# A hybrid decoder layer on one core: where attention's masks, evictions, second q layout and matmul order are placed

## The chip, the cores and the metric

The kernel runs on one core of a Trainium2 chip. The metric is the device time of one execution in microseconds (us): 2123.47 us is the median of three runs of the kernel before (2120.73 to 2124.99). Every number that explains the time comes from one more execution, taken with the hardware profiler.

The engines are named as in the profile: PE is TensorE (matmuls), PEld its weight loads, DVE is VectorE, ACT is ScalarE, POOL is GpSimd, SP is SyncE, which here issues DMAs. SPq, POOLq and so on are the queues of these engines. L1547 is line 1547 of the kernel's source.

## The reference

One decoder layer over 2048 positions of width 1024. The part that matters here is the attention half of the mixer: 8 heads of 64, each with three causal branches of 128-key windows at dilation 1, 4 and 16, which are combined by their softmax denominators.

```python
h = rms_norm(x, g_mix); z = h @ w_in            # 1024 -> 3072
u, gb, gc, q, k, v = split(z)                   # six parts of 512
y_conv = gb * short_conv(gc * u, conv_w)        # depthwise, width 3
q = rms_norm(q, g_q) * 64 ** -0.5; k = rms_norm(k, g_k)
for window, dil in ((128, 1), (512, 4), (2048, 16)):
    # query t attends to keys t, t - dil, ..., t - window
    o[g], lse[g] = softmax_attention(...)
y_attn = sum_g softmax_g(lse)[g] * o[g]
x = x + concat(rms_norm(y_conv), rms_norm(y_attn)) @ w_out
h = rms_norm(x, g_ffn)
x = x + (silu(h @ w_gate) * (h @ w_up)) @ w_down     # 1024 -> 2816 -> 1024
```

All inputs are float32. The kernel splits each operand of a matmul into a high and a low float16 part and adds three products (high x high, high x low, low x high).

## The kernel before

**Stages.** First x is normalised, split and transposed, and one quarter of the convolution's channels is done (0 to 104 us of the profiled execution). Then comes the projection to q, k and v (`project`, to 370 us): four groups g of two heads, four units of 512 positions each, four PSUM banks a unit. Then attention (to about 730 us), with the other three quarters of the convolution and the first two pairs of the output projection threaded between its matmuls; then the output stage (`out_b`, to about 900 us), and the feed-forward part (to the end).

**Projection.** A unit fills four banks with 48 matmuls of 192 columns each (L1249). ScalarE copies each bank to `f` (L1264), squares, and casts v; VectorE and GpSimd normalise (L1304 to L1316); `qkhl` receives the high and low parts (L1319 to L1322), and one DMA writes it to `d_qk` (L1323). `qkhl` and the scratch `row` exist once. The banks come from the pool `cvx`, four banks in turn; the pool `psmm` with three more serves the convolution (and later the output) and is idle here. Beside this, ScalarE, VectorE, GpSimd and SP prepare the weights of later stages (`operands`, `spill_conv`, `spill_out`).

**Attention.** For each pair of heads, `load_pair` reads q, k-high and k-low with twelve transposing DMAs. Then for each head come three branches b in the order 1, 2, 0 (dilations 4, 16, 1). A branch has 16 query tiles of 128, taken four at a time; a step is one PSUM bank of scores, of up to four 128 x 128 blocks with keys on the partitions. Branches 0 and 1 need two steps for four query tiles, branch 2 one: 160 steps in all. In a step TensorE computes the scores (L1534); for b < 2 VectorE adds a mask to the bank (L1539; -1e30 where the band excludes a pair); ScalarE takes the exponential into `sm` (L1541); for b = 2 GpSimd zeroes the excluded half of it with one select (L1543); ScalarE casts to float16 (L1546), VectorE subtracts to get the low part (L1547), both into `et`; TensorE multiplies with v (AV, L1552) into the bank `av`. After four query tiles ScalarE copies `av` to the tile `u` (L1556, L1559). Branches 1 and 2 write `u` to DRAM and read it back in the order of positions as `r` (L1566 to L1571); when branch 0 is done, `combine` adds the three and divides (L1487 to L1495, on GpSimd but for the last head) and writes `d_y`.

Branches 1 and 2 take q in another order of positions, the tile `q16`. `regroup` makes it from the loaded q with four GpSimd copies a head (L1445).

**Order.** The source is written in program order; a planner then puts each engine's instructions into its queue. It runs a simulated clock with costs of its own, and gives each free engine the earliest-written instruction that is ready on that clock, so a later-written one may go first. Engines run their queues strictly in order on the chip. `issue_after(ins)` adds an edge: what the block issues on the engine of `ins` stands behind `ins` in its queue. `attention_pairs` interleaves: after step n of attention it takes 1.95 steps from `fill` (one step is three 512-column matmuls of the convolution or output projection, with the vector work between), and holds them behind the AV matmuls of step n - 12. Where scores and AV stand between these is left to the planner.

**Output stage.** It runs in eight pairs p of position tiles. `out_a(p)` loads x of two tiles into a slot `xk` and adds the convolution's half of the output projection (L599, L602); `tiles(p)` adds the other half (L660), stores the sum (L663) and prepares the feed-forward input. `out_a(p + 2)` stands ahead of `tiles(p)` in the program. The slots are two tiles named `qT` and two named `kb`; p = 1, 4, 7 use `kb`, the others `qT`.

Of the kernel before, what the change touches and what calls it, by code (L numbers as in the profile page):

```python
# [18 lines left out]
P = 128  # L19
# [7 lines left out]
HD = 64  # L27
# [3 lines left out]
class Builder:  # L31
# [170 lines left out]
    def run(self):  # L202
        tc, nc, A = self.tc, self.nc, self.A
        with ExitStack() as ctx:
# [16 lines left out]
            self.dmin = cp.tile([P, 11], F32, name="dmin")  # L221
# [350 lines left out]
    def out_a(self, p):  # L572
# [8 lines left out]
        xk = self.qk.tile([P, 2, D], F32, name="kb" if p % 3 == 1 else "qT")  # L581
# [429 lines left out]
class Fast(Builder):  # L1011
# [6 lines left out]
    PLAIN = 4  # L1018
# [16 lines left out]
    def in_and_conv(self):  # L1035
# [3 lines left out]
        self.d_wc = [dr.tile([P, 3, 2, KC, P], F16, name=f"d_wc{j}") for j in range(3)]  # L1039
        self.d_qk = [dr.tile([S, 6 * P], F16, name=f"d_qk{g}") for g in range(4)]  # L1040
        with ExitStack() as c:
            e = c.enter_context
            self.tmp = e(tc.tile_pool(name="tmp", bufs=3))
            s0 = e(tc.tile_pool(name="s0", bufs=2))
# [40 lines left out]
            self.sums_of = [None] * 4  # L1085
            wanted = [(c, t) for c in range(4) for t in range(2)] if self.PLAIN < 4 else []
            n = -1
            for step in self.conv_steps(0, W, before):
# [3 lines left out]
                if n == 6:  # L1092
                    norms.close()
                    with tc.issue_after(self.act.ins):
                        nc.scalar.preload_act_table_set("natural_log_exp_and_others")
                    self.ring = e(tc.tile_pool(name="ring", bufs=8, side="right"))
                    with tc.issue_after(self.dve.ins), tc.issue_after(self.sp.ins):
                        Wn = self.operands(0)
                elif self.PLAIN == 1 and n in (8, 10):
                    with tc.issue_after(self.dve.ins):  # L1100
                        self.sums(*wanted.pop(0), s0)
# [5 lines left out]
            for g in range(4):  # L1107
                Wg = Wn
                for i in range(4):
                    with ExitStack() as behind:  # L1110
                        for m in self.marks:
                            behind.enter_context(tc.issue_after(m))
                        if g < self.PLAIN:
                            for _ in range(2 if self.PLAIN == 1 else 1):
                                if wanted:
                                    self.sums(*wanted.pop(0), s0)
# [10 lines left out]

    def sums(self, c, t, s0):

        nc = self.nc
        pool, name = ((s0, "s0"), (self.qk, "qT"), (self.qk, "ka"), (self.qk, "kb"))[c]
        if t == 0:
            self.sums_of[c] = [pool.tile([P, 2, 2, 4, 256], F16, name=name, bufs=2) for _ in range(2)]
        Sc = self.sums_of[c]
        xh, xl = self.x[c]
        y = []
        for i in range(2):
            o = slice((t + 2 * i) * P, (t + 2 * i + 1) * P)  # L1140
            y.append(self.tmp.tile([P, KC, P], F32, name="t4"))
            nc.gpsimd.tensor_tensor(y[i], xh[:, :, o], xl[:, :, o], op=ALU.add)
        a11, a12, a21, a22 = (y[i][:, 4 * k:4 * k + 4] for i in range(2) for k in range(2))
        v = nc.vector
        v.tensor_tensor(a22, a21, a22, op=ALU.add)
        v.tensor_tensor(a21, a11, a21, op=ALU.subtract)
        v.tensor_tensor(a11, a22, a11, op=ALU.subtract)
        v.tensor_tensor(a12, a12, a11, op=ALU.subtract)
        for i in range(2):
            src = y[i].rearrange("p (a k) t -> p a k t", a=2)  # L1150
            hi, lo = (Sc[i][:, :, q, :, t * P:(t + 1) * P] for q in range(2))
            nc.scalar.copy(hi, src)
            v.tensor_tensor(lo, src, hi, op=ALU.subtract)

    def operands(self, g):
# [18 lines left out]
        W = [None] * 7  # L1174
# [6 lines left out]
        p = nc.gpsimd  # L1181
        if g < self.PLAIN:
            for n, x in ((0, b11), (1, b21), (2, b12), (3, b22)):
                split(n, x)
            return W
        split(0, b11)
        p.tensor_tensor(b11, b12, b11, op=ALU.subtract)
        split(2, b22)
        p.tensor_tensor(b12, b22, b12, op=ALU.subtract)
        p.tensor_tensor(b22, b22, b11, op=ALU.subtract)  # L1190
        split(5, b22)
        split(4, b11)
        split(1, b21)
        p.tensor_tensor(b21, b21, b22, op=ALU.subtract)
        split(6, b12)
        split(3, b21)
# [26 lines left out]
    def project(self, g, c, W):  # L1223
# [5 lines left out]
        Sc = self.sums_of[c]  # L1229
# [9 lines left out]

        def s_(i, a, t):  # L1240
            return lambda q, k: Sc[i][:, a, q, k, t * P:(t + 1) * P]
# [16 lines left out]
        if g < self.PLAIN:  # L1258
            for i in range(2):
                for h in range(2):  # L1260
                    ps = self.cvx.tile([P, 512], F32, name="cvx")[:, 0:384]
                    for k in range(2):
                        product(ps, lambda t: x_(i, 4 * k, t), W[2 * h + k], k == 0, k == 1)
                    nc.scalar.activation(block(i, h), ps, AF.Copy, scale=u)  # L1264
                last_squares() if i == 0 else None
        else:
            pool, name = ((self.psmm, "mm"), (self.cvx, "cvx"))[self.units % 2]
            self.units += 1
            ps = [pool.tile([P, 512], F32, name=name)[:, 0:384] for _ in range(3)]
            f11, f12, f21, f22 = (block(i, h) for i in range(2) for h in range(2))  # L1270
            left = (lambda t: x_(0, 0, t), lambda t: x_(0, 4, t), lambda t: s_(0, 1, t), lambda t: x_(1, 4, t),
# [663 lines left out]
```

## Time and profile before

| | |
|---|---|
| median of three runs | 2123.47 us (2120.73 to 2124.99) |
| the profiled execution | 2120.25 us, span 2118.5 us |
| TensorE busy | 2024.2 us (96%), 13368 matmuls |
| VectorE busy | 1354.1 us (64%) |
| ScalarE busy | 1031.3 us (49%) |
| GpSimd busy | 686.1 us (32%) |
| mean granted TensorE clock | 0.989 |

A row of a group of instructions reads: line, engine, operation, output <- inputs, shapes, count | busy us, mean ns of one | idle us of the engine just before them, and what ended that idle time. A row of waits reads: engine, tile and line <- who was waited for: us in total, times, longest. A row of a timeline reads: start us, length, engine, line, operation, count, and in brackets the idle time before it and what ended it.

### The profile page before, as it was taken

The numbers are of one execution on the slowest core, as the hardware profiler recorded it, in microseconds if no ns is written. First come the engines' busy times: TensorE is split into PE (matmuls) and PEld (weight loads), VectorE is DVE, ScalarE is ACT, GpSimd is POOL, SyncE is SP. The second block draws the span as 40 slices with busy tenths as digits, with TensorE's granted clock in tenths as the row PEclk, the third lists the DMA queues.
The fourth block names the chain that finished last, engine by engine and source line by source line (L and its number), as shares of the span: only waits on it lengthen the run. The fifth ranks groups of instructions, "written<-read, shape, count | busy, mean of one in ns | idle before, by whom it ended". The sixth has DMA issues, their size and how long they took to land. (4 is left out here: it accounts for less than half of the span.)

```text
span 2118.5 us, 34421 instructions
## 1 busy us (share of the span) xinstructions
PE 2024.2 (96%) x13368; PEld 1122.3 (53%) x13368; DVE 1354.1 (64%) x2487; ACT 1031.3 (49%) x1876; POOL 686.1 (32%) x574
## 2 busy tenths in 40 slices
PE   3999989999998898989999999999999999999998
PEld 2499989566656543434444444444444444444443
DVE  7454453577778867876767676676668575555463
ACT  7446564677777666553434333334333344343341
POOL 0024556334433212222211212231223245555463
PEclk9999999999999999999999999999999999999999
DMA  9658955357856577995323223322332762431442
GB/s 243 151 147 197 225 167 165 101 157 152 181 156 202 152 209 237 252 287 152 119 100 105 86 89 105 115 85 95 110 100 90 273 238 60 140 119 56 149 139 82
DMA packets 460157, 317.00 MB, mean 150 GB/s; under 512 B 255568, under 2 KB 413264, under 8 KB 457808
## 3 DMA queue, kind: packets, MB, share of 16 engines
q1 hardware_dynamic: 442304, 291.56, 49.7%
q10 hardware_dynamic: 17680, 23.16, 3.1%
q8 instruction: 106, 1.74, 0.3%
q14 instruction: 67, 0.55, 0.1%
HBM read 157.96 MB, written 116.85 MB: 130 GB/s over the span
## 5 line engine op out<-in xcount | busy, mean ns | idle before, releaser
L812 PEld LDWEIGHTS <-w 128*128 128x128 f16 x3696 | 362.0, 98 | 452.1 <-issue 17.6
L812 PE MATMUL ps<-b,w 128*128 128x512 f16 x2112 | 466.4, 381 | 11.0 <-DMA b<-d_h 5.2
L945 PE MATMUL ps<-b,w 128*128 128x512 f16 x1848 | 399.7, 379 | 2.9 <-DVE x L953 1.6
L812 PE MATMUL ps<-hb,w 128*128 128x512 f16 x1584 | 347.1, 379 | 0.0
L945 PEld LDWEIGHTS <-w 128*128 128x128 f16 x1848 | 180.6, 98 | 221.8 <-issue 4.0
L1249 PE MATMUL cvx<-w,b 128*128 128x192 f16 x3072 | 256.7, 247 | 8.6 <-ACT f L1264 8.4
L1249 PEld LDWEIGHTS <-b 128*128 128x128 f16 x3072 | 255.4, 98 | 9.9 <-issue 9.3
L705 POOL TENSOR_TENSOR t<-wq 128x512 f32<-128x512 f32 (+1 forms) x46 | 59.7, 1297 | 411.1 <-issue 175.8
L818 DVE TENSOR_TENSOR s<-ps,s 128x512 f32<-128x512 f32 x220 | 150.0, 682 | 36.6 <-PE ps L812 36.1
L952 POOL TENSOR_TENSOR x<-x,s 128x512 f32<-128x512 f32 x72 | 102.9, 1430 | 170.3 <-DVE s L966 132.0
L1547 DVE TENSOR_TENSOR et<-sm,et 128x512 f16<-128x512 f32 (+1 forms) x160 | 128.3, 820 | 36.2 <-ACT et L1546 35.0
L1541 ACT ACTIVATE sm<-s,bound,kap 128x512 f32<-128x512 f32 (+1 forms) x160 | 116.7, 754 | 45.1 <-DVE s L1539 37.7
L953 DVE SCALAR_TENSOR_TENSOR x<-ps,a_u,x 128x512 f32<-128x512 f32 x96 | 71.8, 749 | 98.6 <-PE ps L945 72.1
L191 PE MATMUL mm<-b,wq 128*128 128x512 f16 x320 | 123.3, 385 | 0.0
L192 PE MATMUL mm<-b,wq 128*128 128x512 f16 x320 | 123.1, 385 | 0.0
L193 PE MATMUL mm<-b,wq 128*128 128x512 f16 x320 | 123.0, 384 | 0.0
L722 ACT CAST w<-t 128x512 f16<-128x512 f32 x88 | 53.7, 615 | 127.6 <-PE ps L812 62.0
L96 DVE TENSOR_REDUCE vm_a<-wq 128x1 f32<-128x2048 f32 (+2 forms) x32 | 77.3, 2416 | 52.0 <-DMA wq<-in_w_up_dram 24.4
L1552 PE MATMUL av<-v,et 128*128 128x65 f16 x1800 | 81.5, 194 | 19.1 <-DVE et L1547 12.8
L933 DVE TENSOR_TENSOR w<-t,w 128x512 f16<-128x512 f32 (+1 forms) x96 | 75.4, 802 | 36.7 <-ACT w L932 36.3
L1539 DVE TENSOR_TENSOR s<-s,mask 128x512 f32<-128x512 f32 (+1 forms) x128 | 79.5, 649 | 28.9 <-PE s L1534 24.2
L923 ACT ACTIVATE wq<-wq,asf 128x512 f32<-128x512 f32 x88 | 56.6, 711 | 84.9 <-DMA wq<-d_a 84.9
(290 smaller groups left out, 3206.4 us busy)
## 6 DMA issues: line engine op xcount, KB each, us to landing
d_a<-a ACTq DMA_DIRECT2D x88, 256.0 KB, 2.0
d_wd<-w SPq DMA_DIRECT2D x77, 256.0 KB, 2.0
wq<-d_a SPq DMA_DIRECT2D x64, 256.0 KB, 4.2
b<-d_wd SPq DMA_DIRECT2D x14, 1024.0 KB, 6.6
wq<-in_w_in_dram SPq DMA_DIRECT2D x24, 512.0 KB, 7.2
d_qk<-qkhl SPq DMA_DIRECT2D x16, 768.0 KB, 4.4
d_h<-hl SPq DMA_DIRECT2D x24, 512.0 KB, 3.2
wq<-in_w_gate_dram SPq DMA_DIRECT2D x22, 512.0 KB, 5.3
```

The lines of the kernel that those rows point to most:

```text
L191: self.pe = mm(ps, lhsT=lh(k), rhs=rh(k), start=k == ks[0], stop=False)
L192: mm(ps, lhsT=lh(k), rhs=rl(k), start=False, stop=False)
L193: mm(ps, lhsT=ll(k), rhs=rh(k), start=False, stop=k == ks[-1])
L812: nc.tensor.matmul(ps[self.BANK[n]], lhsT=w[:, x, k], rhs=b[:, y, k], start=first and k == 0 and q == 0, stop=k == 3 and q == 2, skip_grou ...
L818: nc.vector.tensor_tensor(t, x, y, op=ALU.add)
L945: nc.tensor.matmul(ps[self.BANK[n]], lhsT=L[n][:, x, f], rhs=B[n][:, f, y], start=first and f == 0 and q == 0, stop=f == n_f - 1 and q == ...
L952: nc.gpsimd.tensor_tensor(o, o, s_, op=ALU.add)
L1249: self.pe = nc.tensor.matmul(ps[:, 192 * t:192 * (t + 1)], lhsT=lh(x, k), rhs=w[:, y, k], start=start and t + k + q == 0, stop=stop and k ...
L1539: nc.vector.tensor_tensor(sp[:, 0:o], sp[:, 0:o], self.masks[b][:, 512 - o:512], op=ALU.add)
L1541: nc.scalar.activation(e, sp[:, 0:o], AF.Exp, scale=self.kap, bias=self.bound)
L1547: nc.vector.tensor_tensor(et[:, 1], e, et[:, 0], op=ALU.subtract)
L1552: self.pe_av = nc.tensor.matmul(av[:, us.index(u)], lhsT=p_, rhs=v_, start=n_ == 0, stop=n_ == len(ops) - 1)
```

## The change

1. The projection's banks alternate between `cvx` and `psmm`, seven in turn.
2. x slots: odd pairs use `kb`, even pairs `qT`.
3. The unit's q part of `qkhl` is also written to a new DRAM tensor `d_q16` in the order of branch 2, with eight DMAs a unit; `load_pair` reads `q16` from it with four more transposing DMAs a pair. `regroup` goes.
4. The mask add on VectorE goes. After the exponential GpSimd zeroes the excluded entries of branches 0 and 1 with two selects a step, one over the blocks of each kind; the mask tiles and their preparation go.
5. VectorE copies `av` to `u` instead of ScalarE.
6. TensorE's order in attention is written out: scores of step n, AV of step n - 3, then the step's share of `fill`, each held behind the one before by `issue_after`. What follows a branch's last AV (store, read back, combine) moves with it. `et` has five buffers instead of four.
7. `combine` works on 8 query tiles at a time instead of 16, and stores `d_y` in halves; `dmin` has a column for each, `uv` two buffers.
8. Code that was not reached before (`PLAIN`, `sums` and the seven-product form of the projection) is removed.

```diff
-        xk = self.qk.tile([P, 2, D], F32, name="kb" if p % 3 == 1 else "qT")
+        xk = self.qk.tile([P, 2, D], F32, name="kb" if p % 2 else "qT")
...
+        for i in range(2):
+            for h in range(2):
+                pool, name = ((self.cvx, "cvx"), (self.psmm, "mm"))[self.units % 7 % 2]
+                self.units += 1
+                ps = pool.tile([P, 512], F32, name=name)[:, 0:384]
+                for k in range(2):
+                    product(ps, lambda t: x_(i, 4 * k, t), W[2 * h + k], k == 0, k == 1)
+                nc.scalar.activation(block(i, h), ps, AF.Copy, scale=u)
...
+        for a in range(8):
+            nc.sync.dma_start(self.d_q16[g].rearrange("(r c j a) e -> c a r j e", r=NT, c=4, j=4)[c, a],
+                              hl[16 * a:16 * a + 16, :, 0:2].rearrange("p j i x d -> p j (i x d)"))
...
-        st.setdefault("q16", [None, None])
...
+        st["q16"] = self.q16.tile([P, 2, NT, P], F16, name="q16", bufs=2)
+        for r in range(0, NT, 4):
+            self.transpose(st["q16"][:, :, r:r + 4].rearrange("p h r a -> p h (r a)"), self.d_q16[g][P * r:P * (r + 4)])
...
-                    if b < 2:
-                        nc.vector.tensor_tensor(sp[:, 0:o], sp[:, 0:o], self.masks[b][:, 512 - o:512], op=ALU.add)
...
-                    if b == 2:
-                        nc.gpsimd.affine_select(e, e, pattern=[[0, 4], [1, P]], compare_op=ALU.is_ge, fill=0.0, base=0,
-                                                channel_multiplier=-1)
-                    et = self.ep.tile([P, 2, 512], F16, name="et", bufs=4)[:, :, 0:o]
+                    bl = e.rearrange("p (n c) -> p n c", c=P)
+                    d0 = o // P % 2
+                    for m, sg in ((bl, 1),) if b == 2 else ((bl[:, 1 - d0::2], 1), (bl[:, d0::2], -1)):
+                        pattern = [[0, m.shape[1]], [sg, P]]
...
+                        nc.gpsimd.affine_select(m, m, pattern=pattern, compare_op=ALU.is_ge, fill=0.0, base=0,
+                                                channel_multiplier=-sg)
+                    et = self.ep.tile([P, 2, 512], F16, name="et", bufs=5)[:, :, 0:o]
...
-                    nc.scalar.copy(Ub[:, us[0]:us[0] + 4], av)
+                            nc.vector.tensor_copy(Ub[:, us[0]:us[0] + 4], ps)
...
+                    late.append(output)
+                    self.turn = mark.ins
+                    if len(late) > 3:
+                        with self.tc.issue_after(self.turn):
+                            late.pop(0)()
+                        self.turn = self.pe_av.ins
+                    yield self.turn
...
-            for _ in self.attn_steps(g, sts[g], sts[g + 1]):
-                marks.append(self.pe_av.ins)
-                with self.tc.issue_after(marks[n - lag]) if n >= lag else nullcontext():
+            for mark in self.attn_steps(g, sts[g], sts[g + 1]):
+                with self.tc.issue_after(mark):
                     while done < self.RATE * (n + 1):
-                        next(fill, None)
+                        if next(fill, 0) != 0:
+                            self.turn = self.pe.ins
                         done += 1
```

`output` is the function that now holds AV, the eviction, the stores and `combine` of a step; it is called three steps later.

More of the change, by code (lines that the diff above doesn't have):

```diff
@@ L220, in run @@
             self.eps = cp.tile([P, 3], F32, name="eps")
-            self.dmin = cp.tile([P, 11], F32, name="dmin")
+            self.dmin = cp.tile([P, 18], F32, name="dmin")
             self.low = cp.tile([P, 1], F32, name="low")
@@ L1039, in in_and_conv @@
         self.d_wc = [dr.tile([P, 3, 2, KC, P], F16, name=f"d_wc{j}") for j in range(3)]
+        self.d_q16 = [dr.tile([S, 2 * P], F16, name=f"d_q16{g}") for g in range(4)]
         self.d_qk = [dr.tile([S, 6 * P], F16, name=f"d_qk{g}") for g in range(4)]
@@ L1257, in last_squares @@
                 self.squares(3, self.last, self.pstr.tile([P, 4], F32, name="tr"), False)
[L1258 to L1271, printed above, removed]
-                    lambda t: s_(1, 1, t), lambda t: s_(0, 0, t), lambda t: s_(1, 0, t))
-            def plus(o, bank, z):
-                nc.vector.scalar_tensor_tensor(o, bank, u, z, op0=ALU.mult, op1=ALU.add)
-            for m in self.ORDER:
-                product(ps[self.BANK[m]], left[m], W[m], m in (0, 5, 4), m in (1, 2, 3))
-                if m == 0:
-                    nc.scalar.activation(f21, ps[0], AF.Copy, scale=u)
-                elif m == 5:
-                    plus(f12, ps[1], f21)
-                elif m == 1:
-                    nc.scalar.activation(f11, ps[0], AF.Copy, scale=u)
-                    last_squares()
-                elif m == 6:
-                    plus(f22, ps[1], f21)
-                    plus(f22, ps[2], f22)
-                elif m == 3:
-                    plus(f21, ps[1], f21)
-                elif m == 2:
-                    plus(f12, ps[2], f12)
+        for i in range(2):
[6 more added lines that the diff above has]
+                nc.scalar.activation(block(i, h), ps, AF.Copy, scale=u)
+            last_squares() if i == 0 else None
         fi = f.rearrange("p h j d -> p (h j) d")
@@ L1465, in attn_steps, with combine @@
         nc = self.nc
-        uv = self.at.tile([P, 1], F32, name="uv")
+        uv = self.at.tile([P, 1], F32, name="uv", bufs=2)
         nc.vector.tensor_scalar_mul(uv, self.uq[:, g:g + 1], 2.0 ** 17)
-        U, R = {}, {}
+        U, R, late = {}, {}, self.late
         for h, b in [(h, b) for h in range(2) for b in (1, 2, 0)]:
             q, ka, kl = (st[x][:, h] for x in ("qT", "ka", "kl"))
-            q16 = st["q16"][h]
-            if (h, b) == (0, 2):
-                self.regroup(st, 1)
+            q16 = st["q16"][:, h]
             if (h, b) == (1, 1) and g < 3:
                 self.load_pair(g + 1, nx)
-            if (h, b) == (1, 0) and g < 3:
-                self.regroup(nx, 0)
             Vb = self.load_v(g, h, b)
             last = g == 3 and h == 1
-            def combine(c, n):
+            def combine(c, n, h=h, last=last):
                 ts = slice(c, c + n)
@@ L1575, in pools @@
+                    late.append(output)
+                    self.turn = mark.ins
+                    if len(late) > 3:
+                        with self.tc.issue_after(self.turn):
+                            late.pop(0)()
+                        self.turn = self.pe_av.ins
+                    yield self.turn
+        if g == 3:
+            for output in late:
+                output()
     def pools(self, e):
@@ L1585, in constants @@
         nc = self.nc
-        self.masks = []
-        for b in range(2):
-            mask = self.keep.tile([P, 512], F32, name=f"mask{b}")
-            nc.gpsimd.memset(mask, 0.0)
-            for x in range(4):
-                sg = 1 if x % 2 else -1
-                t = mask[:, x * P:(x + 1) * P].rearrange("p (x a) -> p x a", x=4)
-                pattern = [[32 * sg, 4], [sg, 32]] if b == 0 else [[sg, 4], [4 * sg, 32]]
-                nc.gpsimd.affine_select(t, t, pattern=pattern, compare_op=ALU.is_ge, fill=-1e30, base=0,
-                                        channel_multiplier=-sg)
-            self.masks.append(mask)
         self.kap = self.keep.tile([P, 1], F32, name="kap")
```

137 lines of the change are left out of this document (46 added, 91 removed).

## The prediction

> **What bounds the kernel now.** I cut the span into the kernel's stages first, then asked TensorE alone what it waited for. A row of the first view has the stretch, its length, and each engine's busy time with its instructions; the last columns are granted clock, DMA share and GB/s.
>
> ```profile
> 104.00:370.00 266.00, 257.41 (x3083) 256.26 (x3081) 124.57 (x259) 152.46 (x280) 126.80 (x114) 0.99 0.72 179
> 384.00:730.00 346.00, 323.78 (x3631) 212.93 (x3630) 265.28 (x460) 247.95 (x476) 117.10 (x94) 0.99 0.64 160
> 730.00:920.00 190.00, 179.22 (x808) 79.78 (x807) 146.94 (x296) 118.95 (x213) 41.43 (x38) 0.96 0.84 235
> 920.00:2119.00 1199.00, 1180.66 (x5452) 532.95 (x5450) 754.21 (x1293) 446.56 (x790) 388.24 (x303) 1.00 0.38 123
> ```
>
> TensorE sets the end in every stage: it is busy 257 of 266 us in the projection, 324 of 346 in attention, 179 of 190 in the output stage. The change adds and removes no matmul, so all it can give is idle time of TensorE and the slow clock behind it. The last row, over half of the span, is untouched by the diff. The view of who waited for whom, TensorE alone:
>
> ```profile
> PE av L1552 <- DVE et L1547: 12.8, 17, 2.7
> PE cvx L1249 <- ACT f L1264: 8.4, 4, 4.8
> PE mm L191 <- DVE qT L599: 7.0, 1, 7.0
> PE av L1552 <- ACT et L1546: 3.8, 8, 1.6
> ```
>
> Three places, then: the projection waits 8.4 us for a bank, attention 12.8 + 3.8 = 16.6 us for probabilities (of 346.0 - 323.8 = 22.2 us idle), the output stage once 7.0 us for a sum with x.
>
> **Seven banks.** TensorE's rows of the projection:
>
> ```profile
> 113.18 150.64 PE L1249 MATMUL cvx<-w,b 128*128 128x192 f16 x1824
> 277.25 33.87 PE L1249 MATMUL cvx<-w,b 128*128 128x192 f16 x384 [4.75 <-ACT f L1264]
> ```
>
> Undisturbed, 150.64 / 1824 = 0.0826 us per matmul; a bank takes 48, so 3.96 us, and four banks cover a ScalarE that is 16 us late, seven 28 us. The longest wait beyond four is 4.75 us, less than the 11.9 us that three banks add: all 8.4 us can go. After it 384 matmuls took 33.87 instead of 31.7 us: 2.1 us of slow clock. Together 10.5 us.
>
> **x slots by pair.** The output stage's rows, by TensorE, the DMA queue and GpSimd:
>
> ```profile
> 815.74 0.38 PE L192 MATMUL ps<-b,b 128*128 128x512 f16 x1
> ...
> 817.90 0.38 PE L193 MATMUL ps<-b,b 128*128 128x512 f16 x1
> 825.25 0.58 PE L191 MATMUL mm<-b,b 128*128 128x512 f16 x1 [6.97 <-DVE qT L599]
> ...
> 830.32 0.63 PE L191 MATMUL ps<-b,b 128*128 128x512 f16 x1
> ...
> 788.03 0.85 SPq L663 DMA_DIRECT2D d_x<-kb  x1
> ...
> 812.27 1.26 SPq L663 DMA_DIRECT2D d_x<-qT  x1
> ...
> 819.57 0.82 SPq L592 DMA_DIRECT2D qT<-in_x_dram  x2
> ...
> 823.38 2.28 POOL L602 TENSOR_TENSOR qT<-qT,xt 128x512 f32<-128x512 f32 x1 [20.46 <-DMA qT<-in_x_dram]
> ```
>
> The x of pair 5 goes into the slot of pair 2, which is stored at 812.27; the load is issued at 819.57, GpSimd and VectorE get it at 823.4, TensorE stands for 6.97 us. Then 12 matmuls take 830.32 - 825.25 = 5.07 us, where ten took 2.16 before: 2.5 us of slow clock, 9.5 us in all. By parity, pair 5 takes the slot of pair 1, whose last stores went out at 788, 24 us earlier, and from pair 4 on every load waits only for the pair four before it. Pair 7 loads later than now, behind pair 3's store, still a pair ahead of its use. VectorE is busy 147 of 190 us here, so something else may be late by a microsecond or two next: I take 8.0 of 9.5.
>
> **Masks, evictions.** Groups of attention's stretch, by line; behind the bar busy us, mean ns, idle before:
>
> ```profile
> L1541 ACT ACTIVATE sm<-s,bound,kap 128x512 f32<-128x512 f32 x120 | 91.1, 782 | 27.5 <-DVE s L1539 25.0 <-PE s L1534 1.8 <-DVE et L1547 0.3
> L1546 ACT CAST et<-sm 128x512 f16<-128x512 f32 x120 | 72.1, 624 | 2.4 <-POOL sm L1543 1.3 <-POOL cu L1405 0.5 <-PE av L1552 0.2
> L1539 DVE TENSOR_TENSOR s<-s,mask 128x512 f32<-128x512 f32 x88 | 58.9, 690 | 17.1 <-PE s L1534 16.6
> L1539 DVE TENSOR_TENSOR s<-s,mask 128x384 f32<-128x384 f32 x40 | 21.4, 557 | 11.8 <-PE s L1534 7.6 <-ACT et L1546 4.2
> L1559 ACT COPY u<-av 128x260 f32<-128x260 f32 x64 | 23.9, 375 | 18.1 <-PE av L1552 17.7
> L1445 POOL COPY q<-qT 128x512 f16<-128x512 f16 x24 | 29.6, 1276 | 5.2 <-PE s L1534 5.2
> L1543 POOL TENSOR_SCALAR_AFFINE_SELECT sm<-sm 128x512 f32<-128x512 f32 x32 | 21.8, 684 | 67.9 <-ACT sm L1541 60.2 <-DVE cg L1415 7.6
> L1487 POOL TENSOR_TENSOR r<-r,r 128x1040 f32<-128x1040 f32 x7 | 17.9, 2554 | 87.9 <-DMA r<-d_u 87.9
> L1488 POOL TENSOR_TENSOR u<-u,r 128x1040 f32<-128x1040 f32 x7 | 17.7, 2524 | 4.3 <-ACT u L1559 3.2 <-POOL r L1487 0.9
> L1495 POOL TENSOR_TENSOR u<-u,bm 128x1024 f32<-128x1024 f32 x7 | 14.3, 2049 | 18.8 <-DVE bm L1493 18.8
> L1405 POOL MEMSET cu<- 128x2 f32 x2 | 0.2, 92 | 0.0
> ```
>
> VectorE loses the mask adds, 58.9 + 21.4 = 80.3 us. It gains 96 evictions of 260 columns: from 690 and 557 ns for 512 and 384 columns, 1.04 ns a column, so 557 - 124 x 1.04 = 428 ns, 41 us (ScalarE's 375 ns is the other end, 36 us). Net -39 us of 265. ScalarE loses 96 x 0.375 = 36 of 248 us.
>
> GpSimd gains two selects for each of 128 score tiles. No row shows one of 256 columns: if all of 684 ns is width it is 0.34 us, if all is fixed 0.68. The memset of two columns, 92 ns, is the nearest to a fixed part: 0.092 + 0.592 / 2 = 0.39 us, 0.24 for 128 columns. So 88 x 0.78 + 40 x 0.63 = 94 us, less 29.6 us of regrouping copies: GpSimd goes from 117 to 181 of 346 us. No engine is full; the question is who waits for whom. GpSimd runs in order, and each combine (L1487, L1488, L1495, 49.9 us in seven) now stands between masks.
>
> GpSimd and VectorE also hold each other up. The timelines of GpSimd and VectorE:
>
> ```profile
> 601.95 2.58 POOL L1488 TENSOR_TENSOR u<-u,r 128x1040 f32<-128x1040 f32 x1
> ...
> 571.10 0.74 DVE L1411 SCALAR_TENSOR_TENSOR cg<-cu,convw,cg 128x512 f32<-128x512 f32 x1
> ...
> 596.84 0.68 DVE L1547 TENSOR_TENSOR et<-sm,et 128x512 f16<-128x512 f32 x1
> ...
> 602.22 2.87 DVE L1411 SCALAR_TENSOR_TENSOR cg<-cu,convw,cg 128x512 f32<-128x512 f32 x1
> ```
>
> L1411, 0.74 us elsewhere, takes 2.87 us and ends at 605.09, 0.56 us behind GpSimd's add (604.53). L1547's mean of 795 ns in the groups above its 0.68 us alone is the same. That is where TensorE's 16.6 us come from: the probabilities of a step stand behind a combine.
>
> The Trainium skill's page SBUF — State Buffer, in "Who interferes with whom", says that a VectorE instruction with two SBUF inputs and a GpSimd instruction that reads SBUF exclude each other for the whole instruction, and one with a single SBUF input is free. By it the mask add (PSUM and mask) never blocked, and the selects that replace it do. The row above agrees for an add on GpSimd, with 0.18 us of overlap; the price for selects is the third rival.
>
> **TensorE's order.** AV of a step now comes three steps behind its scores. A step is 346 / 160 = 2.16 us, so 6.5 us are there for exponential 0.78, two selects 0.78, cast 0.62, subtraction 0.68: 2.9 us, leaving 3.6 us. The longest wait for L1547 was 2.7 us, so the 16.6 us can go. The three half-combines (half of 2.55 + 2.52 + 2.05: 3.6 us) just fit; a little more wait for r or for L1493 does not. I charge 0.6 us for each of seven, 4.1 us: attention gains 12.5 us. Bounds: all 22.2 idle us and the 1% of clock missing there (3.5 us) on one side, the rivals on the other. The 5.6 us of other idle time I leave; three banks of scores and two of AV are reused after three and two steps, later than their 0.78 and 0.43 us need.
>
> **q stored twice.** Rows of the page's DMA part, then the DMA queue, then GpSimd and the queue at the end of the projection:
>
> ```profile
> d_qk<-qkhl SPq DMA_DIRECT2D x16, 768.0 KB, 4.4
> ...
> 406.31 2.91 SPq L1566 DMA_DIRECT2D d_u<-u  x4
> ...
> 473.98 6.12 SPq L199 DMA_TRANSPOSE qT<-d_qk  x4
> ...
> 354.80 8.91 POOL L1445 COPY q<-qT 128x512 f16<-128x512 f16 x8
> ...
> 385.75 1.31 POOL L1322 TENSOR_TENSOR qkhl<-row,qkhl 128x256 f16<-128x256 f32 x2
> ...
> 390.69 0.88 SPq L1455 DMA_DIRECT2D v<-d_v  x2
> ```
>
> Per unit eight more issues at 2.91 / 4 = 0.73 us or less: up to 5.8 us of a queue that serves a unit every 4 x 3.96 = 15.8 us, ahead of the weight loads and spills written behind them. They are hidden by the 28 us of banks; without that cover a late weight reduction costs up to 5.8 us each time. Four more transposes a pair cost 6.1 us of queue, a pair ahead of their use. At the end of the projection the v load of attention stands behind the last unit's stores (385.75 + 1.31, then 390.69), now up to 5.8 us more, while TensorE arrives 10 us sooner; against that GpSimd is rid of the 8.91 us of copies that held up the last two units. From 0 to 6 us of wait, near its lower end: 2.0 us, charged to the projection, which gives 8.5. uv, dmin, the tile of five, the halved d_y stores and the missing mask tiles touch nothing that waits.
>
> **Sum.** 8.5 + 8.0 + 12.5 = 29.0 us from the profiled execution's 2120.25 us (span 2118.5 and 1.75 around it): 2091.3. The median of the runs lies 3.2 us above that execution, so 2094.
>
> **Rivals.** (a) Attention gives nothing, since in-order queues trade one wait for another: 2094 + 12.5 = 2107. For it: GpSimd, ScalarE and VectorE become one chain. Against: 3.6 us of slack and less work on two of them. (b) Projection and x slots give nothing: 2094 + 16.5 = 2111. For it: DMA share 0.72 there and eight more stores a unit. Against: their causes are a bank and a slot. (c) Slower: selects and VectorE's two-input work take turns. In a step of branches 0 and 1 they need 2s + 0.68 + (49.9 + 24 x 0.74) / 160 = 2s + 1.10 us against TensorE's 323.8 / 160 = 2.02. At 0.39 us that is 1.88, just below; at 0.684 it is 2.47, so 128 x 2.47 + 32 x 2.02 = 381 us, 35 longer, less 16.5: 2142. It decides from 0.62 us on, where 363 us are reached. (d) Slower too: the planner puts the add of the r tiles (L1487) ahead of the masks of branch 0, where it waits 87.9 / 7 = 12.6 us for its DMA; each costs 12.6 - 3.6 = 9.0 us, 63 in all, less 16.6 and 16.5: 2153. It decides from 8.3 us of wait on. For it: that wait exists; against: only planned order can place it so early, and r is now planned later too.
>
> **Chances.** Forecast 0.61, (a) 0.15, (b) 0.10, (c) 0.08, (d) 0.06. The range goes from all gains (10.5 + 9.5 + 22.2 + 3.5 = 45.7 below 2123.5: 2078) to 2118, over (a) and (b), and leaves out (c) and (d). A change of 0.2%, 4.2 us, is what can be told: faster 0.81, same 0.07 (where (a) and (b) meet), slower 0.12.
>
> **What would show it.** Right: no wait of L1249 for L1264 over 1 us; no wait of L191 for L599; attention's stretch near 333 us; selects of 256 columns near 0.39 us. Wrong: AV waiting for et by more than 16 us in all, GpSimd idle behind r while masks queue, L1547's mean over 1 us, or the first AV waiting for v or for q's transposes.

## The result: slower, and where the time went

The changed kernel takes 2140.59 us, the kernel before 2122.1 us on the same chip: a ratio on record of 1.0091 (the two medians alone give 1.0087), with a 95% interval of 1.0079 to 1.0103. The forecast was 2094. The profiled executions are 2140.6 and 2118.5 us long, 22.1 us apart. The view by stretches, cut at five marks of TensorE (the projection's first and last matmul, the first and the last AV matmul, the first FFN matmul); a row has the stretch, its length, the busy time of TensorE, its weight loads, VectorE, ScalarE and GpSimd, then granted clock, DMA share and GB/s. The changed kernel:

```profile
103.80:368.20 264.40, 257.10 (x3081) 255.91 (x3081) 120.87 (x257) 150.01 (x274) 117.29 (x106) 0.99 0.76 190
368.20:408.50 40.30, 21.65 (x97) 10.08 (x96) 9.98 (x21) 15.01 (x30) 14.08 (x20) 0.75 0.67 168
408.50:754.50 346.00, 319.71 (x3598) 213.06 (x3597) 224.43 (x449) 221.64 (x370) 198.27 (x336) 0.97 0.65 158
754.50:918.40 163.90, 157.00 (x716) 70.24 (x716) 123.29 (x248) 98.63 (x179) 36.08 (x35) 0.99 0.77 231
```

The same marks in the kernel before:

```profile
104.10:370.10 266.00, 257.41 (x3082) 256.26 (x3081) 124.47 (x259) 152.46 (x280) 126.80 (x114) 0.99 0.72 179
370.10:393.40 23.30, 22.57 (x117) 11.08 (x116) 9.69 (x21) 11.39 (x25) 11.87 (x13) 1.00 0.44 119
393.40:728.80 335.40, 314.95 (x3578) 208.06 (x3577) 258.91 (x449) 242.42 (x466) 114.05 (x89) 0.98 0.64 159
728.80:895.40 166.60, 157.27 (x714) 70.35 (x715) 125.43 (x255) 99.94 (x182) 35.09 (x34) 0.97 0.80 227
```

Two stretches carry the loss. From the projection's end to the first AV it is 40.3 us instead of 23.3 (+17.0), with TensorE idle nearly half of it and its clock at 0.75. From the first to the last AV it is 346.0 instead of 335.4 (+10.6). Three stretches give little: projection -1.6, output stage -2.7, FFN -0.9 us (1222.2 and 1223.1); the first AV as a whole comes 15.1 us later. Six rows of TensorE's waits in the changed kernel say the same (total, times, longest; the waits before the projection are left out):

```profile
PE s L1448 <- DMA q<-d_q: 18.7, 1, 18.7
PE av L1475 <- DVE et L1465: 13.6, 12, 3.0
PE av L1475 <- ACT et L1464: 12.3, 7, 3.5
PE ps L812 <- ACT s L863: 5.5, 1, 5.5
PE mm L1194 <- ACT f L1210: 4.3, 3, 3.1
PE cvx L1194 <- ACT f L1210: 2.2, 2, 1.4
```

**Ahead of attention.** The first scores wait once, 18.7 us, for q16. The DMA queue and TensorE at that point:

```profile
388.55 2.99 SPq L1246 DMA_DIRECT2D d_q<-qkhl  x5
392.88 5.27 SPq L199 DMA_TRANSPOSE q<-d_q  x4
401.05 0.38 PE L1448 MATMUL s<-q,ka 128*128 128x256 f16 x1 [18.65 <-DMA q<-d_q]
```

The transposes of pair 0's q16 are issued behind the last unit's last stores, although pair 0's q was stored some 190 us earlier. The tile of q16 has doubled from two buffers of 4 KB a partition to two of 8 KB, and in the built program its pool now reaches over the memory of the projection's qkhl.

**In attention.** GpSimd, VectorE and TensorE around one of seven like places:

```profile
524.94 1.96 POOL L1461 TENSOR_SCALAR_AFFINE_SELECT sm<-sm 128x256 f32<-128x256 f32 x4
530.96 2.52 POOL L1400 TENSOR_TENSOR r<-r,r 128x520 f32<-128x520 f32 x2 [4.06 <-DMA r<-d_u]
533.43 0.77 POOL L1461 TENSOR_SCALAR_AFFINE_SELECT sm<-sm 128x256 f32<-128x256 f32 x2
534.88 1.12 DVE L1465 TENSOR_TENSOR et<-sm,et 128x512 f16<-128x512 f32 x1 [5.97 <-ACT et L1464]
534.91 0.30 PE L1475 MATMUL av<-v,et 128*128 128x65 f16 x4 [3.49 <-ACT et L1464]
521.92 0.41 SPq L1495 DMA_DIRECT2D d_u<-u  x1
526.71 0.37 SPq L1497 DMA_DIRECT2D r<-d_u  x1
```

GpSimd stands 4.06 us before the add of the r tiles, then does both halves (2.52 us), and only then comes the next mask, whose exponentials ScalarE had finished by 528.8 at the latest. AV runs three steps later now, so branch 2's u goes out at 521.92, its r is fetched from 526.71, and the add stands in GpSimd's order at about the time it lands. GpSimd's waits for r add up as follows:

```profile
POOL r L1400 <- DMA r<-d_u: 17.7, 7, 5.1
```

The evictions came out at their estimate (424 ns, 428 forecast), the selects above it: 486 and 412 ns in the mean for 256 and 128 columns where 0.39 and 0.24 us were forecast, so the new selects take 115 us in that stretch instead of 94 (its groups; mean ns behind the busy time):

```profile
L1461 POOL TENSOR_SCALAR_AFFINE_SELECT sm<-sm 128x256 f32<-128x256 f32 x213 | 99.3, 486 | 83.8 <-ACT sm L1453 80.1 <-DVE cg L1334 2.1 <-DVE et L1465 1.4
L1461 POOL TENSOR_SCALAR_AFFINE_SELECT sm<-sm 128x128 f32<-128x128 f32 x38 | 15.6, 412 | 0.0
L1483 DVE COPY u<-av 128x260 f32<-128x260 f32 x63 | 26.7, 424 | 13.6 <-PE av L1475 13.0
```

### The profile page after: what moved, and what is told of

Its sections match the earlier page's. It is cut to its first block, busy times and chain, and to the rows that moved or that the text cites. A ratio compares the mean times of both kernels' runs of the same rounds, so it can differ in the third digit from the quotient of the medians.

```text
span 2140.6 us, 34957 instructions
## 1 busy us (share of the span) xinstructions
PE 2027.0 (95%) x13368; PEld 1126.0 (53%) x13368; DVE 1320.6 (62%) x2483; ACT 1012.5 (47%) x1780; POOL 760.4 (36%) x809
## 4 chain that ended last, share of the span: by engine, by line
PE 65%; DMA 9%; DVE 7%; ACT 6%; SPq 5%; issue 4%; POOL 2%; DVEq 0%; ACTq 0%; POOLq 0%
PE ps L812 33%; PE ps L945 15%; SPq L199 3%; PE mm L191 3%; PE mm L192 3%; PE mm L193 3%; PE s L1448 2%; PE cvx L1194 2%; PE mm L1194 2%; PE av L1475 2%; DVE vm_a L96 1%; DMA nx_x<-in_x_dram 1%; DMA wq<-d_a 1%; DMA x<-d_x 1%; POOL sm L1461 1%
## 5 line engine op out<-in xcount | busy, mean ns | idle before, releaser
L812 PE MATMUL ps<-b,w 128*128 128x512 f16 x2112 | 465.9, 381 | 11.3 <-ACT s L863 5.5
L1461 POOL TENSOR_SCALAR_AFFINE_SELECT sm<-sm 128x256 f32<-128x256 f32 (+2 forms) x288 | 136.3, 495 | 143.2 <-ACT sm L1453 137.9
L1465 DVE TENSOR_TENSOR et<-sm,et 128x512 f16<-128x512 f32 (+1 forms) x160 | 121.2, 762 | 99.6 <-ACT et L1464 98.0
L1194 PE MATMUL cvx<-w,b 128*128 128x192 f16 x1776 | 151.2, 246 | 3.3 <-ACT f L1210 2.2
L1464 ACT CAST et<-sm 128x512 f16<-128x512 f32 (+1 forms) x160 | 93.8, 589 | 71.3 <-POOL sm L1461 70.2
L191 PE MATMUL mm<-b,wq 128*128 128x512 f16 x320 | 125.7, 393 | 0.0
L192 PE MATMUL mm<-b,wq 128*128 128x512 f16 x320 | 125.7, 393 | 0.0
L193 PE MATMUL mm<-b,wq 128*128 128x512 f16 x320 | 125.6, 392 | 0.0
L1194 PE MATMUL mm<-w,b 128*128 128x192 f16 x1296 | 113.0, 248 | 4.3 <-ACT f L1210 4.3
L1475 PE MATMUL av<-v,et 128*128 128x65 f16 x1800 | 85.4, 195 | 26.1 <-DVE et L1465 13.6
```

What stands on the lines that cost most here:

```text
L191: self.pe = mm(ps, lhsT=lh(k), rhs=rh(k), start=k == ks[0], stop=False)
L192: mm(ps, lhsT=lh(k), rhs=rl(k), start=False, stop=False)
L193: mm(ps, lhsT=ll(k), rhs=rh(k), start=False, stop=k == ks[-1])
L812: nc.tensor.matmul(ps[self.BANK[n]], lhsT=w[:, x, k], rhs=b[:, y, k], start=first and k == 0 and q == 0, stop=k == 3 and q == 2, skip_grou ...
L1194: self.pe = nc.tensor.matmul(ps[:, 192 * t:192 * (t + 1)], lhsT=lh(x, k), rhs=w[:, y, k], start=start and t + k + q == 0, stop=stop and k ...
L1461: nc.gpsimd.affine_select(m, m, pattern=pattern, compare_op=ALU.is_ge, fill=0.0, base=0, channel_multiplier=-sg)
```

## Experiments

For each run: the ratio to the kernel before with its interval, the times of the marks in its profiled execution (us from the span's start), and the sum of AV's waits for et.

| run | ratio (95%) | projection ends | first AV | last AV | first FFN matmul | AV waits for et |
|---|---|---|---|---|---|---|
| before | 1 | 370.1 | 393.4 | 728.8 | 895.4 | 16.6 |
| changed | 1.0091 (1.0079 to 1.0103) | 368.2 | 408.5 | 754.5 | 918.4 | 25.9 |
| e1 | 1.0057 (1.0043 to 1.0072) | 369.6 | 396.7 | 746.2 | 909.0 | 26.2 |
| e2 | 1.0050 (1.0036 to 1.0065) | 368.0 | 406.9 | 742.0 | 908.1 | 21.5 |
| e3 | 1.0005 (0.9996 to 1.0014) | 360.1 | 395.4 | 731.7 | 899.1 | 17.5 |
| e4 | 1.0000 (0.9990 to 1.0010) | 371.8 | 395.5 | 731.2 | 895.2 | 19.7 |
| e5 | 1.0006 (0.9996 to 1.0017) | 371.0 | 398.3 | 733.9 | 897.7 | 22.1 |
| e7 | 1.0156 (1.0134 to 1.0177) | 360.5 | 393.4 | 773.8 | 936.8 | 48.4 |
| e8 | 0.9983 (0.9973 to 0.9992) | 360.2 | 385.0 | 732.5 | 895.3 | 26.8 |
| e9 | 0.9865 (0.9846 to 0.9884) | 360.7 | 384.8 | 709.4 | 873.0 | 9.3 |
| e10 | 1.0047 (1.0030 to 1.0064) | 371.5 | 398.6 | 747.1 | 909.9 | 26.9 |
| e11 | 0.9876 (0.9859 to 0.9892) | 373.8 | 392.5 | 714.8 | 878.1 | 8.0 |
| e12 | 0.9995 (0.9984 to 1.0007) | 370.3 | 408.9 | 733.7 | 898.6 | 7.9 |
| e13 | 0.9881 (0.9864 to 0.9897) | 361.0 | 385.5 | 710.2 | 877.1 | 8.7 |

The FFN stage, which no run changes, lasts between 1218.2 and 1230.5 us in these executions; times of single executions are compared only by their marks up to there.

### e1: q16 over free memory

```diff
             early.close()
+            e(tc.tile_pool(name="pad", bufs=1)).tile([P, 3104], F32, name="pad")
             self.fq = e(tc.tile_pool(name="fq", bufs=1))
+            self.hlp = e(tc.tile_pool(name="hlp", bufs=1))
...
-        self.qkhl = self.fq.tile([P, 4, 6, 2, HD], F16, name="qkhl")
+        self.qkhl = self.hlp.tile([P, 4, 6, 2, HD], F16, name="qkhl")
```

> The changed kernel with q16's two buffers laid over memory that is free before the last unit of the projection (a pad behind tmp, qkhl above the other tiles of fq). Nothing else is moved. Theory: the first scores wait 18.7 us for q16 because its memory lies on qkhl, which the last unit still stores from; then the first scores start at 382 to 386 instead of 401, the first AV waits up to 5 us for v, and the kernel takes 13 to 19 us less: 2122 to 2128. Rival: the eight stores per unit hold up the DMA queue itself; then the first scores stay behind 395 and at most 6 us are gained: 2134 or more.

Measured: 2136.9 us beside 2124.93. The pad shifts the projection's other tiles of that pool too, but of these only qkhl shared memory with q16. The place in memory was the cause of that wait: the transposes go out from 364.7 us on and the first scores start at 384.3 instead of 401.1. But the first AV gains only 11.8 us and the kernel some 7 by the ratios, because the next wait is close behind. TensorE and ScalarE:

```profile
384.33 0.27 PE L1450 MATMUL s<-q,ka 128*128 128x256 f16 x1
394.92 0.37 PE L1450 MATMUL s<-q,ka 128*128 128x256 f16 x1 [6.19 <-ACT sm L1455]
391.38 0.71 ACT L1241 CAST qkhl<-row 128x256 f16<-128x256 f32 x2 [6.38 <-DMA d_q<-qkhl]
394.19 0.67 ACT L1455 ACTIVATE sm<-s,bound,kap 128x384 f32<-128x384 f32 x1 [0.36 <-DMA d_v<-vs]
```

Three banks of scores are full and wait for the first exponential, which stands in ScalarE's order behind the last unit's casts. Attention now waits for the tail of the projection on ScalarE.

### e2: the r-add later in GpSimd's order

```diff
-                e.tensor_tensor(X[1], X[1], X[2], op=ALU.add)
+                with self.tc.issue_after(self.sel):
+                    e.tensor_tensor(X[1], X[1], X[2], op=ALU.add)
...
-                        nc.gpsimd.affine_select(m, m, pattern=pattern, compare_op=ALU.is_ge, fill=0.0, base=0,
-                                                channel_multiplier=-sg)
+                        self.sel = nc.gpsimd.affine_select(m, m, pattern=pattern, compare_op=ALU.is_ge, fill=0.0, base=0,
+                                                           channel_multiplier=-sg).ins
```

> The changed kernel with the add of the r tiles (L1400) queued on GpSimd behind the masks of the third step of the next head. Theory: GpSimd stands for r's DMA (17.7 us in 7 waits) with masks queued behind it, and that is most of AV's 26.1 us of waiting for et; then that sum falls under 10 us, no wait of GpSimd for r is over 1 us, and the kernel takes 12 to 22 us less: 2118 to 2128. Rival: the combine's 7.8 us of GpSimd work a head doesn't fit between the masks wherever it stands; then the sum stays over 18 us and the gain is under 6 us: 2134 or more.

Measured: 2134.47 us beside 2124.93. The wait for r is as good as gone (one of 1.9 us), the stretch from first to last AV is 335.1 us instead of 346.0, but AV still waits 21.5 us. Both expectations were half right: the wait for r cost some 9 to 11 us, and what was left has another cause. VectorE and GpSimd at one place:

```profile
573.80 1.17 DVE L1405 TENSOR_SCALAR bm<-u 128x8 f32<-128x8 f32 x1
575.75 1.26 DVE L1405 TENSOR_SCALAR bm<-u 128x8 f32<-128x8 f32 x1
577.92 1.42 DVE L1466 TENSOR_TENSOR et<-sm,et 128x512 f16<-128x512 f32 x1
572.09 2.86 POOL L1402 TENSOR_TENSOR u<-u,r 128x520 f32<-128x520 f32 x2
575.72 1.26 POOL L1346 TENSOR_TENSOR sq<-sq,c 128x512 f32<-128x512 f32 x1
```

The two halves of the combine stand back to back on GpSimd, VectorE's small steps for both stand between two subtractions, and in each half one of them (L1405) ends only with the GpSimd instruction beside it. The subtraction for AV, whose cast was ready at 576.4 (ScalarE's row, 575.78 and 0.62 us), starts at 577.9 and takes 1.42 us.

### e3: seven banks alone

```diff
-                    ps = self.cvx.tile([P, 512], F32, name="cvx")[:, 0:384]
+                    pool, name = ((self.cvx, "cvx"), (self.psmm, "mm"))[self.units % 7 % 2]
+                    self.units += 1
+                    ps = pool.tile([P, 512], F32, name=name)[:, 0:384]
```

> The kernel before with the seven banks alone. The prediction's term: the waits for L1264 go and 8 to 10.5 us with them: 2112 to 2114 beside 2122. Theory now: the planner, which knows of seven banks, lets ScalarE's evictions fall behind by as many banks (the largest lag was 17 us in the kernel before, 29.7 us in the changed one), so that waits of 4 to 8 us stay: 2116 to 2122.

Measured: 2126.42 us beside 2124.93, no difference. Both expectations fell. The waits for L1264 did go (0.7 us in all is left) and the projection's matmuls end 10.0 us sooner, as the prediction had it. Then the gain is handed back. TensorE and ScalarE:

```profile
393.29 0.37 PE L1536 MATMUL s<-q,ka 128*128 128x256 f16 x1 [6.12 <-ACT sm L1543]
395.41 0.82 PE L1554 MATMUL av<-v,et 128*128 128x65 f16 x12 [1.11 <-DMA v<-d_v]
386.42 1.14 ACT L1322 CAST qkhl<-row 128x512 f16<-128x512 f32 x2 [0.64 <-POOL row L1318]
392.56 1.23 ACT L1543 ACTIVATE sm<-s,bound,kap 128x384 f32<-128x384 f32 x2 [0.48 <-DMA d_qk<-qkhl]
```

The first AV comes at 395.4, and at 393.4 in the kernel before. TensorE's 8.4 us of waits in the projection were slack: the last unit's way through ScalarE, GpSimd and the DMA queue is no shorter with more banks, it only lags TensorE by more (ScalarE ends the last eviction at 376.2 us, at 374.4 in the kernel before; from the end of a bank's last matmul to the start of its eviction the timelines show up to 23.9 us, 17.2 before).

### e4: x slots alone

```diff
-        xk = self.qk.tile([P, 2, D], F32, name="kb" if p % 3 == 1 else "qT")
+        xk = self.qk.tile([P, 2, D], F32, name="kb" if p % 2 else "qT")
```

> The kernel before with the x slots by parity alone. The prediction's term: the 7.0 us wait for L599 goes and 8.0 to 9.5 us with it: 2112 to 2114 beside 2122. Rival, from the changed kernel, whose output stage is 2.8 us shorter: another wait takes its place and 1 to 4 us are gained: 2118 to 2121.

Measured: 2125.72 us beside 2124.93, no difference. The wait of 7.0 us for L599 is gone, but the output stage is only 2.6 us shorter (five waits of 0.5 to 2.4 us in its place), and that goes too where the FFN starts. There the wait for the scale of L863 is longer; this run:

```profile
PE ps L812 <- ACT s L863: 5.5, 1, 5.5
```

The kernel before:

```profile
PE ps L812 <- ACT s L863: 2.1, 1, 2.1
```

### e5: e1 and e2 together (both diffs above)

> The changed kernel with both e1's place for q16 and e2's later r-add. Theory: the two losses lie in different stretches and add up: first AV at 396 to 398 us, last AV some 335 us later, 2122 to 2128, level with the kernel before. Rival: what is gained ahead of attention is lost in it again; then 2131 or more.

Measured: 2125.06 us beside 2124.46, level with before, as the theory had it. The two losses are in different places and add up.

### e7: q16 by GpSimd's copies again

```diff
-        for a in range(8):
-            nc.sync.dma_start(self.d_q16[g].rearrange("(r c j a) e -> c a r j e", r=NT, c=4, j=4)[c, a],
-                              hl[16 * a:16 * a + 16, :, 0:2].rearrange("p j i x d -> p j (i x d)"))
...
+            if (h, b) == (0, 2):
+                self.regroup(st, 1)
...
+            if (h, b) == (1, 0) and g < 3:
+                self.regroup(nx, 0)
```

> The changed kernel with q16 made by GpSimd's copies again (no second store of q, no transposes of it); banks, x slots, masks and order as changed. Theory: the first AV comes when the last unit's chain through ScalarE, GpSimd and the DMA queue is through, at 393 to 397 us with or without seven banks, so 15 us of the loss ahead of attention go; in attention the 29.6 us of copies come back to GpSimd beside the masks and AV's wait for et stays at 20 to 30 us: 2124 to 2132. Rival: the lag of the evictions (largest 29.7 us) delays the first AV without the stores too: then it stays behind 402 us, and 2133 or more.

Measured: 2158.55 us beside 2124.46, the slowest run of all; the expectation of the time was wrong by 27 us. The first half of the theory held: without the stores the projection ends at 360.5 and the first AV comes at 393.4. The price in attention was far too low. GpSimd's waits for r and its rows at a block of copies:

```profile
POOL r L1407 <- DMA r<-d_u: 27.2, 7, 5.3
...
508.35 5.28 POOL L1365 COPY q<-qT 128x512 f16<-128x512 f16 x4 [0.71 <-PE s L1455]
513.58 2.88 POOL L1468 TENSOR_SCALAR_AFFINE_SELECT sm<-sm 128x512 f32<-128x512 f32 x5
```

Four copies hold five masks for 5.28 us, and GpSimd stands for r 27.2 us instead of 17.7. How the 48.4 us of AV's waits divide between the two was not tried. In this kernel q on GpSimd beside the masks costs more than its second store does; with the combines placed otherwise (e9) it was not tried.

### e8 and e10: the second store of q

e8 adds to e1 a second buffer of qkhl and stores q16 in four transfers of 128 partitions instead of eight of 16:

```diff
-        hl = self.qkhl
+        hl = self.qkhls[c % 2]
...
-        for a in range(8):
-            nc.sync.dma_start(self.d_q16[g].rearrange("(r c j a) e -> c a r j e", r=NT, c=4, j=4)[c, a],
-                              hl[16 * a:16 * a + 16, :, 0:2].rearrange("p j i x d -> p j (i x d)"))
+        for j in range(4):
+            nc.sync.dma_start(self.d_q16[g].rearrange("(r c j a) e -> c j a r e", r=NT, c=4, j=4)[c, j],
+                              hl[:, j, 0:2].rearrange("p i x d -> p (i x d)"))
```

> e1 with two buffers of qkhl, taken in turn by the units, and the second store of q in four transfers a unit instead of eight. Theory: after e1 the first AV (396.7 us) waits for ScalarE, which stands twice (4.6 and 6.4 us) before it may write qkhl again, until the nine stores of the unit before have read it; then the first AV comes at 385 to 391 us and the kernel takes 6 to 11 us less than e1. Rival: the chain of weight loads and reductions of the projection sets the end of ScalarE's work; then the first AV stays behind 394 us and the gain is under 3 us.

Measured: 2120.21 us beside 2124.46; the first AV at 385.0, within the theory's range, and the gain over e1 (some 16 us by the ratios) above it. e10, with the second buffer and the eight transfers, tells the two parts apart:

> e1 with two buffers of qkhl and the second store of q still in eight transfers a unit. Theory: the single buffer, held through nine stores, is what kept ScalarE and GpSimd waiting; then this run stands within 4 us of e8 (2120 beside 2124.5 before) and the projection's matmuls end near 360 us. Rival: the number of transfers on the DMA queue is the cause; then the projection ends behind 366 us as in e1 (369.6) and the run stands 8 to 13 us above e8.

Measured: 2136.09 us beside 2125.26, as e1. The theory of the single buffer fell: with eight transfers a second buffer gives nothing. The rival holds: with two buffers, the transfers are the cause; four transfers with one buffer were not tried. Projection and first AV come 11.3 and 13.6 us sooner with four. Their length per issue (min/median/max ns), eight a unit and then four a unit:

```profile
L1249 SPq DMA_DIRECT2D d_q<-qkhl x128: 315/430/2017, 136.9 to 397.1; - x128
```

```profile
L1249 SPq DMA_DIRECT2D d_q<-qkhl x64: 593/610/1870, 136.7 to 381.2; - x64
```

The queue in e10, where weights of the output projection, prepared beside the next unit, stand behind the stores:

```profile
247.02 1.46 SPq L1249 DMA_DIRECT2D d_q<-qkhl  x3
...
249.02 3.17 SPq L1249 DMA_DIRECT2D d_q<-qkhl  x5
...
259.48 2.12 SPq L1280 DMA_DIRECT2D t<-in_w_out_dram  x2
```

The same load in e8:

```profile
248.70 1.97 SPq L1280 DMA_DIRECT2D t<-in_w_out_dram  x2
```

The weight load goes out 10.8 us later with eight transfers. One unit's stores are not enough for that: the two groups above take 4.6 us, e8's for this unit 3.3. The delay grows over the units: the first unit's stores start 0.2 us later than in e8, the third's 1.2, the fifth's 5.3, the seventh's 9.7. The load's reduction, VectorE's and ScalarE's work on it and the evictions written behind that work follow, in the order of their engines. The chain that ended last in the changed kernel runs this way and not through TensorE; its pieces there (start, us, what):

```profile
287.64 0.74 SPq L1295
...
289.81 7.21 DMA t<-in_w_out_dram
297.04 1.22 DVE vm_a L96
```

Whether it is the number of the transfers or their shape (16 partitions each) that makes the queue late was not taken apart.

### e9 and e12: the combines spread

e9 is e8 with each combine cut into its steps, one of them behind the mask and the subtraction of each further step of the next head:

```diff
-                            combine(0, 8)
-                            combine(8, 8)
+                            (r0, u0, i0, y0), (r1, u1, i1, y1) = combine(0, 8), combine(8, 8)
+                            self.todo += [r0, u0, i0, r1, y0, u1, i1, y1]
...
+                    if self.todo:
+                        with self.tc.issue_after(sel), self.tc.issue_after(sub):
+                            self.todo.pop(0)()
```

> e8 with the seven combines spread: each of their six GpSimd instructions and their VectorE steps behind the masks and subtraction of a further step of the next head, one a step. Theory: the adds in pairs and VectorE's steps that wait for them are what is left of AV's waits for et in e2 (21.7 us); then these fall under 8 us and the stretch from first to last AV to under 330 us (346.0 as changed, 335.4 before), 12 to 20 us less than e8. Rival: masks and subtractions alone are too slow for three steps of lateness; then the sum stays over 15 us.

Measured: 2095.6 us beside 2124.46, a ratio of 0.9865: faster than both kernels. AV's waits for et and the stretch from first to last AV:

```profile
PE av L1491 <- DVE et L1478: 8.4, 18, 1.5
PE av L1491 <- ACT et L1477: 0.9, 2, 0.5
...
384.80:709.40 324.60, 313.63 (x3595) 210.69 (x3595) 227.01 (x450) 222.86 (x374) 209.35 (x339) 0.99 0.68 168
```

GpSimd does no less (209 us), but between two masks its other work lasts 1.8 us or less, but for two places of 3.0 us (up to 4.4 as changed, without the wait for r). AV's waits of 9.3 us stay above the expected 8; the gain over e8 (25 us by the ratios) is above the expected 12 to 20. e12 puts the same combines into the changed kernel and leaves q16 where it was:

> The changed kernel with the spread combines alone, q16 where the change has it. Theory: the loss in attention is the combine's alone, so the stretch from the first to the last AV falls from 346.0 to 322 to 328 us and the kernel takes 20 to 25 us less than as changed, with the first AV still at 407 to 409 us: 2116 to 2121 where before is 2124. Rival: part of e9's gain over e8 comes from work that the earlier start let in; then 2124 or more.

Measured: 2124.66 us beside 2125.26. From first to last AV it is 324.8 us, the first AV stays at 408.9; by the ratios (1.0091 and 0.9995) that is 20 us less than as changed. The time itself lies above the range I gave and at the rival's mark of 2124; the kernel before ran at 2125 here. The stretch decides for the theory: it is as short as in e9 (324.6) and 10.6 us shorter than before, so the whole loss in attention went with the combine's place. That e9 gains 25 us over e8, 5 more than this run over the changed kernel, is within the intervals; whether the earlier start adds to it stays open.

### e11 and e13: banks and x slots in the faster kernel

e11 is e9 with `pool, name = self.cvx, "cvx"` in place of the seven banks, e13 is e9 with `p % 3 == 1` for the x slots.

> e9 with four banks in the projection again. Theory: with the first AV at 384.8 us, where scores already wait 4.3 us for ScalarE, the banks are worth only what the chain behind the evictions lets through: the matmuls of the projection end some 9 us later (369 to 371 us), the first AV 3 to 7 us later, and the kernel takes 3 to 7 us more than e9: 2099 to 2103 where before is 2124.5. Rival, the prediction's term in full: 8 to 10 us more. Rival, e3's answer: nothing, within 2 us of e9.

Measured: 2098.54 us beside 2125.26. TensorE waits 8.5 us for L1213 again, the projection ends 13.1 us later, the first AV 7.7, the last AV 5.4; the ratio rises by 0.0011, 2 to 3 us, and the intervals overlap. Expected were some 9, 3 to 7 and, in time, 3 to 7 us. The prediction's full term, 10.5 us, would put the ratio at 0.9914 and is ruled out here too. But the banks are not worth nothing everywhere: with the copies gone and four stores, 7.7 of the 13.1 us reach the first AV.

> e9 with the x slots as before (p % 3 == 1). Theory, from e4: the wait for L599 of some 7 us comes back, and waits in the rest of the output stage and at the first FFN tiles shrink by as much: within 3 us of e9. Rival, the prediction's term: 8 to 9.5 us more than e9.

Measured: 2099.51 us beside 2125.26, a ratio 0.0016 above e9's, some 3 us, and the intervals overlap. The wait for L599 is back (5.0 us). 8 us more than e9 would be a ratio of 0.9903, outside this run's interval.

## Why the prediction was wrong

- **The sum as a method.** The prediction added up TensorE's idle times and called them time of the kernel, stretch by stretch. The banks' term was right in size where it lay and worth nothing at the end (e3); the wait for the x slot went and other waits took its place (e4). Alone, the two come to what rival (b) had forecast. Forecast and measured, from the profiled executions: projection and what lies ahead of the first AV -8.5, came +15.1 (0.3 us of gain before the projection counted in); x slots -8.0, came -2.7, and -3.6 with the FFN; attention -12.5, came +10.6.
- **Seven banks (10.5 us).** The size was right: alone they end the projection 10.0 us sooner (e3). The step that failed is that this reaches the end. The prediction read which wait ends last on TensorE, and not what the first AV waits for: the last unit's chain over ScalarE, GpSimd and the DMA queue, at 393 to 395 us with four banks or seven, as long as GpSimd's copies are there (before, e3, e7).
- **"They are hidden by the 28 us of banks."** The price of the eight issues was right (4.2 us a unit against at most 5.8, 67.5 us in all); the cover wasn't. The queue is what the weight loads wait in, so its lateness comes back through ScalarE's evictions: they lag by up to 29.7 us in the changed kernel (29.6 in e10, 23.6 in e8 with four stores), all seven banks are used up, and 6.5 us of waits for L1210 stay. e8 beside e10 shows it: four transfers instead of eight are worth 14 us by the ratios.
- **The transition (0 to 6 us, taken as 2.0).** It was 18.7 us. The prediction counted issues on the queue and named q's transposes as a place to look, but not why they would be late: the new tile's two buffers, 16 KB in all, reach into memory that the projection's last unit still stores from. A bound for a moved transfer has to include what its target tile lies over.
- **x slots (8.0).** "Something else may be late by a microsecond or two next" was sized too low: 6.6 us of waits took its place in the same stage and 3.4 us at the FFN's first matmuls.
- **Attention (12.5).** This is the fourth rival by its mechanism: the add of the r tiles stands ahead of masks in planned order. Its price was wrong on both sides: r is waited for 2.5 us on average (17.7 in seven, from 0.3 to 5.1), not 12.6, but it decides far below the 8.3 us given as its threshold, since the 3.6 us of slack were already spoken for. "The three half-combines just fit" is the step that failed: they come as pairs (2.5 us for two r-adds), VectorE's steps for both stand ahead of a subtraction, and some of them end only with GpSimd's work. "R is now planned later too" was taken as a reason against; in the trace it is one for it, because AV three steps later also stores u later. The 0.6 us charged for each combine was some 2.9 us (20 us in seven, e12).
- **What held.** Evictions by VectorE 424 ns against 428; selects of 256 columns were not far off, 0.44 us in the median (0.486 in the mean) against 0.39; VectorE's subtraction for 512 columns kept its mean (774 ns as changed, 795 before); and the third rival, selects too slow beside VectorE's work, fell: with the same selects e9 needs 324.6 us from first to last AV, and its first to last AV runs 10.8 us shorter than before. The room that the prediction saw in attention is there; the change alone doesn't reach it.

## What to carry to other kernels

Before an idle time of the busiest engine is counted as a gain, follow what the next stage's first instruction waits for: if that is the tail of other engines, the idle time is slack and will turn up again at the stage's end. When work is moved to an engine whose order is fixed, look at what else stands in that order and how long it can wait, and cut the long pieces so that none stands whole ahead of the new, urgent ones. A tile that grows or a transfer that is split has costs away from its place: the memory it lies over and the queue that later loads share.

## What the runs showed of the hardware

- A `tensor_scalar` on VectorE with one SBUF tensor of 8 columns takes 0.15 us when GpSimd is idle (e2, from 738 us on), and 1.17 and 1.26 us in e2 beside a GpSimd tensor_tensor, ending with it. I had expected only instructions with two SBUF inputs to be held up. The Trainium skill's page SBUF — State Buffer, in "Who interferes with whom", frees an instruction with one SBUF input only "outside the 2-port perf modes", a condition that the prediction left out, and counts `tensor_scalar` among the operations that can enter a mode with both ports and then lock GpSimd out or be locked out for the whole instruction; the rows of e2 agree.
- Halving the transfers of the same bytes, from 16 partitions each to 128, made each issue longer (median 430 to 610 ns) and the queue's time for all of them shorter (71.0 to 47.9 us, summed over the rows of those lines).
- A select in the changed kernel took at least 0.29 us for 128 columns, 0.40 for 256 and 0.63 for 512 (medians 0.31, 0.44 and 0.64). The shortest ones give about 0.17 us fixed and 0.9 ns a column, where the prediction had taken 0.09 us as fixed.
